# Merging the blocks of a triangular inverse earlier and in place, inside a hand-ordered hybrid decoder layer

## The chip, the cores and the metric

The kernel runs on one NeuronCore of a Trainium2 chip. Its metric is the device time of one execution in microseconds (us), the median of several runs. Below, PE is TensorE's matmul, PEld its weight load, DVE VectorE, ACT ScalarE, POOL GpSimd, and SP the queue that issues most DMAs (SPq its issuing instructions).

## The reference

One decoder layer on 512 tokens of width 1024. A normed input is projected once; half of the result goes to block-sparse attention with 8 heads of 64, the other half to a chunked gated DeltaNet with 8 heads of 64; both join in an output projection, and a squared-ReLU MLP of width 4096 follows. The part that matters here is the DeltaNet, with 8 chunks of 64 tokens for each head:

```python
qc, kc, vc = to_chunks(q), to_chunks(k), to_chunks(v)
decay = jnp.exp(jnp.where(causal, g_cum[..., :, None] - g_cum[..., None, :], -jnp.inf))
k_beta = kc * bc[..., None]
m = jnp.where(strict, jnp.einsum('bhnid,bhnjd->bhnij', k_beta, kc) * decay, 0.0)
a_mat = m + jnp.eye(C)
rhs = jnp.concatenate([vc * bc[..., None], k_beta * jnp.exp(g_cum)[..., None]], axis=-1)
uw = lax.linalg.triangular_solve(a_mat, rhs, left_side=True, lower=True, unit_diagonal=True)
u, w = uw[..., :dh], uw[..., dh:]
...
def step(state, xs):
    u_c, w_c, q_c, k_c, a_c, gl = xs
    v_new = u_c - jnp.einsum('bhck,bhkv->bhcv', w_c, state)
    o = jnp.einsum('bhck,bhkv->bhcv', q_c, state) + jnp.einsum('bhcs,bhsv->bhcv', a_c, v_new)
    state = state * gl[..., None, None] + jnp.einsum('bhck,bhcv->bhkv', k_c, v_new)
    return state, o
```

So each 64x64 unit triangular matrix is inverted, applied to the keys and the values, and then a state is carried through the chunks one after the other.

## The kernel before, in words

**Stages.** The input is normed and transposed (`pre_norm`, to about 20 us). The input projection (`projections`) runs 24 items of 128 columns and one wide item of 512, in the order of the string `ORDER`: k, q, v and z are the DeltaNet's pairs of heads 0 to 3, x and y the queries and keys of attention's pairs, and w its values. Each item has 24 products of 128x512 into one of two banks `ps_mm`, three for each of eight slices, since a float32 product is made of high and low halves (`mm3`). A weight slice is loaded into one of two buffers `w_raw` (L200, SP), cast to the high half on ACT (L205), and its low half is made on DVE or POOL (L206; the string `LO` says which). The bank is then evacuated by a stream of its own (`take_k`, `take_q`, `take_v`, `take_z`, `take_a`): for k, q and v a convolution with one pass on ACT (L485) and three on DVE (L488).

**The DeltaNet.** `chunks` makes for each pair of heads the matrices `NT` and `AT`. `inverse` loads the 32x32 diagonal blocks of `NT` through DRAM (`d_n`) with one block on each partition, inverts them by 31 pairs of DVE operations (L880, L881), and stores the inverses to `d_u` and their transposes to `d_t` (L885, L886). `scan` begins with the merge of two 32x32 blocks to one 64x64 inverse: it clears a buffer `UT` (L892, POOL), loads the transposes into `uap` (L897) and the blocks into `UT` (L900), makes 128 products of 32x32 (p1, L909), copies them (L913), makes 128 more (p2, L922), and writes them into `UT` (L926). Then come, for each pair of heads, the keys times a factor, `kB` (L934, POOL, one buffer), and their products with `UT` (L941), from which `LWQ` is filled (L943). The scan itself is eight steps (L981 to L1006), two yields each, in which the state `S` goes through DVE (L999, L1000). `finish_o` norms the outputs, waits for all of z0 to z3, transposes them and writes `mg_h` and `mg_l`.

**Attention.** `scores` and `values` work pair by pair with the keys `kt` (one buffer) and the queries `pt`. `output` then multiplies the joined halves (`mg`, `ma`) with the output weights `wo`; the MLP follows from about 313 us.

**What sets the order.** All of these are Python generators in one planner, `Weave`. Its clock `now` moves on by each product's columns, and each stream says at every yield how long it wants to wait, by a default in `WAIT`, or by an entry of `DELAY` under the stream's name and count ("merge.2" is the second yield of `merge`), or it waits for a mark that another stream sets. Among the streams that are ready the one of the lowest `RANK` goes first. This fixes the order of TensorE's instructions for good. The other engines are ordered by a list scheduler, in which `LEAD` and `PRIO` raise a stream's priority.

`scan` is spawned only when the inverse, the last chunks and all four values are marked, after the projections' pool is closed:

```python
    weave.run({"inverse", "chunks3", "v0", "v1", "v2", "v3"})
    sP.close()
    sc = pool("scan", 2, stack=sA, side="right")
    spawn(RANK["scan"], scan(), LEAD["scan"])
```

`big` buffers (14 of 128x2048) and `big_x` buffers (4 of the same size) are handed on when their last reader is done. `UT`, `inv`, `pt`, `LWQ` are `big`; `picks`, `kraw`, `ma_h`, `ma_l`, and later `mg_h` and `mg_l` are `big_x`.

Of the kernel before, what the change touches and what calls it, by code (L numbers as in the profile page):

```python
# [19 lines left out]
WAIT = {'h': 0.26, 'conv_k': 5.48, 'k': 6.88, 'conv_q': 8.11, 'q': 1.52, 'conv_v': 12.72, 'v': 2.29, 'z': 11.49, 'ab': 0.67, 'g': 9.16, 'scalars': 55.01, 'r_in': 0.0, 'r_out': 30.56, 'kk': 3.56, 'kk_out': 93.91, 'gl': 0.0, 'qk': 13.83, 'va': 1.36, 'a': 6.03, 'row': 1.56, 'rows': 4.29, 'pv': 2.34, 'att': 1.98, 'inverse': 0.76, 'merge': 6.6, 'p1': 2.26, 'p2': 223.99, 'w': 1.15, 'vn': 1.06, 'state': 0.64, 'o_in': 5.67, 'o': 1.23, 'wo': 1.48, 'wo_out': 0.86, 'normed3': 7.36, 'normed': 18.07, 'n': 2.53, 'up': 2.92, 'sums': 0.12, 'turned': 11.21, 'pv0': 3.36, 'wv': 3.58}  # L20

RANK = {'chunks': 5, 'inverse': 3, 'scan': 2, 'scores': 5, 'values': 4, 'finish_o': 2, 'take': 1}
LEAD = {'chunks': 30, 'inverse': 100, 'scan': 100, 'scores': 0, 'values': 0, 'finish_o': 100, 'take': 300, 'take_a': 100}
# [1612 lines left out]
```

## Time and profile before

| | us |
|---|---|
| median of three runs | 636.75 (636.13 to 636.93) |
| the profiled execution, its own time | 639.11 |
| its span, first to last instruction | 637.3 |
| the part ahead of the MLP (`w_up`'s weights in groups 2 to 7, `w_down`) | about 313 |
| TensorE's products, busy | 620.8 |
| VectorE, busy | 484.4 |
| ScalarE, busy | 370.3 |
| GpSimd, busy | 136.1 |

The profiled execution is one run, with 11091 instructions; a stretch's idle TensorE time is the stretch's length less the busy time. A busy TensorE is not always one at full speed: the granted clock is given beside it.

### The profile page before, as it was taken

Reading aid. Unit: us, or ns where it says so; the run is one execution under the profiler, and the core shown is the slowest. Engines: PE = TensorE matmul, PEld = TensorE weight load, DVE = VectorE, ACT = ScalarE, POOL = GpSimd, SP = SyncE. Lnnn points to the kernel's source line nnn. Section 1 sums busy time; section 2 is a strip of 40 time slices with the busy share of each in tenths; the row PEclk is TensorE's granted clock in tenths of the full one; section 3 lists DMA queues with packets and bytes.
Section 4 is the critical chain, followed back from the end, with each engine's and each line's share of the span. In section 5 each row is a group of like instructions: output and inputs, shape, how many; then the busy total and the mean of one; then the engine's idle time right before and its main releaser. Section 6 shows DMA issues by size and latency. Waiting matters only on the chain.

```text
span 637.3 us, 11091 instructions
## 1 busy us (share of the span) xinstructions
PE 620.8 (97%) x4291; PEld 535.8 (84%) x4291; DVE 484.4 (76%) x725; ACT 370.3 (58%) x620; POOL 136.1 (21%) x173
## 2 busy tenths in 40 slices
PE   9999999999989998999999999999999999999996
PEld 8777878888878876888898999999998888887884
DVE  4688887998735777947875578878789888887776
ACT  6385575445748656854325585556755666665661
POOL 4335430011334222002412311231211220000001
PEclk9999999999979999999999999999999999999999
DMA  6421335334371124724399998999999999867503
GB/s 223 131 76 65 101 100 143 107 102 146 113 120 37 41 61 138 247 96 166 117 361 248 175 296 241 255 262 233 280 257 340 298 291 285 261 212 298 180 0 133
DMA packets 61270, 115.26 MB, mean 181 GB/s; under 512 B 15862, under 2 KB 35449, under 8 KB 60834
## 3 DMA queue, kind: packets, MB, share of 16 engines
q1 hardware_dynamic: 43228, 84.93, 40.0%
q0 software_dynamic: 17696, 29.36, 22.1%
q8 instruction: 34, 0.56, 0.4%
q10 hardware_dynamic: 294, 0.27, 0.1%
q14 instruction: 18, 0.15, 0.1%
HBM read 106.65 MB, written 35.15 MB: 222 GB/s over the span
## 4 chain that ended last, share of the span: by engine, by line
PE 81%; DVE 6%; DMA 5%; ACT 3%; POOL 1%; issue 1%; SPq 1%; POOLq 0%; DVEq 0%; ACTq 0%
PE ps_mm L148 40%; PE ps_g L148 22%; PE ps_a L148 16%; DMA wo_raw<-in_w_out 1%; PE ps_a L152 1%; DMA xx<-in_x 1%; PE ps_g L152 1%; DVE conv L488 1%; DMA wd<-d_T 1%; DVE S L999 1%; DMA nb<-in_pre_mix 1%; DMA uap<-d_t 1%; DVE S L1000 1%; POOL oss L243 1%; SPq L900 1%
## 5 line engine op out<-in xcount | busy, mean ns | idle before, releaser
L181 ACT CAST wdh<-wd 128x1024 fp32r<-128x1024 f32 x53 | 55.6, 1050 | 51.2 <-PE ps_mm L148 23.6
L182 DVE TENSOR_TENSOR u_l<-w,u_h 128x1024 fp32r<-128x1024 f32 x46 | 56.2, 1224 | 37.9 <-ACT u_h L181 37.9
L182 DVE TENSOR_TENSOR wdl<-wd,wdh 128x1024 fp32r<-128x1024 f32 x53 | 64.9, 1225 | 22.8 <-ACT wdh L181 22.7
L181 ACT CAST u_h<-w 128x1024 fp32r<-128x1024 f32 x46 | 47.8, 1044 | 57.2 <-PE ps_a L148 19.8
L148 PE MATMUL ps_mm<-hT_h,w_hi 128*128 128x512 f32 (+1 forms) x192 | 76.4, 403 | 0.2 <-ACT hT_h L314 0.2
L148 PE MATMUL ps_mm<-hT_h,w_lo 128*128 128x512 f32 (+1 forms) x192 | 72.9, 385 | 0.0
L148 PE MATMUL ps_mm<-hT_l,w_hi 128*128 128x512 f32 (+1 forms) x192 | 72.6, 383 | 0.0
L1306 POOL DMA_DIRECT2D d_T<-in_w_down x32 | 33.1, 1034 | 143.6 <-DMA d_T<-in_w_down 82.3
L205 ACT CAST w_hi<-w_raw 128x512 fp32r<-128x512 f32 x56 | 34.8, 622 | 37.0 <-PE ps_mm L148 15.9
L206 POOL TENSOR_TENSOR w_lo<-w_raw,w_hi 128x512 fp32r<-128x512 f32 x21 | 27.2, 1294 | 97.2 <-ACT w_hi L205 94.2
L148 PE MATMUL ps_mm<-wdh,u_h 128*128 128x512 f32 x116 | 45.2, 390 | 0.0
L148 PE MATMUL ps_mm<-wdl,u_h 128*128 128x512 f32 x116 | 45.1, 389 | 0.0
L148 PE MATMUL ps_mm<-wdh,u_l 128*128 128x512 f32 x116 | 45.1, 389 | 0.0
L148 PEld LDWEIGHTS ps_mm<-hT_h,w_lo 128*128 128x128 f32 x192 | 35.8, 189 | 7.5
L148 PEld LDWEIGHTS ps_mm<-hT_h,w_hi 128*128 128x128 f32 x192 | 36.0, 190 | 6.6 <-issue 0.5
L148 PEld LDWEIGHTS ps_mm<-hT_l,w_hi 128*128 128x128 f32 x192 | 36.1, 190 | 5.4
L182 DVE TENSOR_TENSOR u_l<-f,u_h 128x1024 fp32r<-128x1024 f32 x28 | 34.1, 1218 | 0.0
L148 PE MATMUL ps_g<-wdh,u_h 128*128 128x512 f32 x80 | 31.2, 390 | 0.4 <-DVE y L1480 0.4
L148 PE MATMUL ps_g<-wdh,u_l 128*128 128x512 f32 x80 | 31.1, 389 | 0.0
L148 PE MATMUL ps_g<-wdl,u_h 128*128 128x512 f32 x80 | 31.1, 389 | 0.0
L206 DVE TENSOR_TENSOR w_lo<-w_raw,w_hi 128x512 fp32r<-128x512 f32 x35 | 24.4, 696 | 8.2 <-ACT w_hi L205 7.1
L488 DVE SCALAR_TENSOR_TENSOR conv<-ps_mm,cw,conv 128x511 f32<-128x511 f32 (+2 forms) x36 | 26.8, 746 | 4.1 <-ACT conv L485 3.4
(461 smaller groups left out, 1867.4 us busy)
## 6 DMA issues: line engine op xcount, KB each, us to landing
d_T<-in_w_down POOLq DMA_DIRECT2D x48, 512.0 KB, 10.8
wd<-d_T SPq DMA_DIRECT2D x32, 512.0 KB, 6.2
w<-in_w_up SPq DMA_DIRECT2D x28, 512.0 KB, 7.7
wd<-in_w_down SPq DMA_DIRECT2D x24, 512.0 KB, 6.7
w_raw<-in_w_in SPq DMA_DIRECT2D x46, 256.0 KB, 2.7
wo_raw<-in_w_out SPq DMA_DIRECT2D x16, 256.0 KB, 2.9
d_T<-d_T POOLq DMA_DIRECT2D x8, 512.0 KB, 11.0
xx<-in_x SPq DMA_DIRECT2D x4, 512.0 KB, 7.4
```

The lines of the kernel that those rows point to most:

```text
L148: nc.tensor.matmul(o, l, r, **kw)
L152: nc.tensor.transpose(o, i, ident[:k, :k])
L181: nc.scalar.copy(hi, src)
L182: tt(lo, src, f32(hi), op=OP.subtract)
L205: nc.scalar.copy(hi, raw)
L206: (sub or tt)(lo, raw, f32(hi), op=OP.subtract)
L243: nc.gpsimd.tensor_tensor(r, r, m, op=OP.pow)
L488: stt(c[:, s:], p[:, :512 - s], cw[:, ft, j:j + 1], c[:, s:], op0=OP.mult, op1=OP.add)
L900: nc.sync.dma_start(z3(UT[32 * b:32 * b + 32, :, :, o:o + 32]), d_u[b].rearrange("z j i -> j z i"))
L999: tt(Sn[hs, :, hs], S[hs, :, hs], EGL[hs, :, n:n + 1].to_broadcast([64, 4, 64]), op=OP.mult)
L1000: tt(Sn[hs, :, hs], Sn[hs, :, hs], sp[n][cs, hh::2], op=OP.add)
L1306: nc.gpsimd.dma_start(d_T[t][k], block(b, second)[k], accum_op=OP.add, max_dma_last_dim=1024)
```

## The change

The merge leaves `scan` and becomes a stream of its own, `merge`, that waits for the mark "inverse"; the products with `kB` become a third stream, `weights_of_k`, that waits for "merged"; `scan` waits for "LW". `UT` is no longer a buffer of its own: once the inverse's two stores have left, its buffer is viewed as `UT`, and the six loads go into it. The lower left quarter, in which p1's result stands until p2 has read it, is cleared afterwards. `kB` gets one `big_x` buffer for all four pairs, and the keys of attention's pairs 1 and 2 another.

```diff
         def ev_k(ps):
-            kts[p] = at.tile([128, 2, 512], FR, name="kt", bufs=1)
+            if p in (0, 3):
+                kts[p] = at.tile([128, 2, 512], FR, name="kt", bufs=1)
+            else:
+                if p == 1:
+                    kt2.append(big_x("kt", (128, 2, 2, 512), FR))
+                kts[p] = kt2[0][:, p - 1]
...
+        merged.append(inv.rearrange("p a j i -> p (a j i)").rearrange("p (h t e) -> p h t e", h=8, t=4))
         iT = iN
         nc.vector.tensor_copy(iT, iU.rearrange("p j i -> p i j"))
...
-    def scan():
-        UT = big("UT", (128, 8, 4, 64))
-        nc.gpsimd.memset(UT, 0.0)
-        uap = [sc.tile([128, 4, 4, 32], FT, name="uap", tag="ot", bufs=4) for _ in range(2)]
+    def merge():
+        yield "inverse"
+        UT = merged[0]
         z3 = lambda a: a.rearrange("p h t i -> p (h t) i")
+        left, right = ([slice(64 * c + o, 64 * c + o + 32) for c in range(2)] for o in (0, 32))
+        first, second = slice(0, 32), slice(32, 64)
         for c in range(2):
-            for z in range(2):
-                nc.sync.dma_start(z3(uap[z][64 * c:64 * c + 32]), d_t[2 * c, 16 * z:16 * z + 16].rearrange("z j i -> j z i"))
-        for b in range(4):
-            o = 32 * (b % 2)
-            nc.sync.dma_start(z3(UT[32 * b:32 * b + 32, :, :, o:o + 32]), d_u[b].rearrange("z j i -> j z i"))
+            nc.sync.dma_start(z3(UT[left[c], :, :, second]), d_t[2 * c].rearrange("z j i -> j z i"))
+        for c in range(2):
+            nc.sync.dma_start(z3(UT[right[c], :, :, second]), d_u[2 * c + 1].rearrange("z j i -> j z i"))
+        for c in range(2):
+            nc.sync.dma_start(z3(UT[left[c], :, :, first]), d_u[2 * c].rearrange("z j i -> j z i"))
         yield WAIT["merge"]
...
             for c in range(2):
-                b = slice(64 * c + 32, 64 * c + 64)
-                nc.scalar.copy(uap[z][b], p1[b])
+                nc.scalar.copy(UT[right[c], zs, :, first], p1[right[c]])
...
             for c in range(2):
-                a = slice(64 * c, 64 * c + 32)
-                nc.scalar.mul(z3(UT[a, 4 * z:4 * z + 4, :, 32:64]), z3(p2[a]), -1.0)
-        yield WAIT["p2"]
+                nc.scalar.mul(UT[left[c], zs, :, second], p2[left[c]], -1.0)
+        for c in range(2):
+            nc.gpsimd.memset(UT[right[c], :, :, first], 0.0)
+        mark("merged", WAIT["p2"])
+
+    def weights_of_k():
+        yield "merged"
+        UT = merged[0]
+        kBs = big_x("kB")
...
-                kB = sc.tile([128, 512], FT, name="kB", bufs=1).rearrange("p (t h e) -> p t h e", t=4, h=2)
+                kB = kBs[:, p].rearrange("p (t h e) -> p t h e", t=4, h=2)
...
+        mark("LW")
+
+    def scan():
+        yield "LW"
+        UT = merged[0]
...
     spawn(RANK["inverse"], inverse(), LEAD["inverse"])
+    spawn(RANK["inverse"], merge(), LEAD["scan"])
+    spawn(RANK["inverse"], weights_of_k(), LEAD["scan"])
```

The planner's numbers are drawn anew as well:

```diff
-RANK = {'chunks': 5, 'inverse': 3, 'scan': 2, 'scores': 5, 'values': 4, 'finish_o': 2, 'take': 1}
-LEAD = {'chunks': 30, 'inverse': 100, 'scan': 100, 'scores': 0, 'values': 0, 'finish_o': 100, 'take': 300, 'take_a': 100}
+RANK = {'chunks': 5, 'inverse': 2, 'scan': 2, 'scores': 2, 'values': 3, 'finish_o': 5, 'take': 1}
+LEAD = {'chunks': 30, 'inverse': 100, 'scan': 300, 'scores': 0, 'values': 30, 'finish_o': 300, 'take': 0, 'take_a': 0}
...
-ORDER = 'k0 k1 q0 q1 q2 k2 q3 k3 x0 y0 z0 w x1 v2 v0 y1 v1 v3 x2 y2 z2 x3 z1 y3 z3'
+ORDER = 'k0 k1 q0 q1 q2 k2 q3 k3 x0 y0 z0 x1 y1 w v2 v1 v0 v3 z2 x2 y2 y3 x3 z1 z3'
...
-LO = 'ppvvpvpvpppvvvvppvvvvvvvvvvvvvvvpvvppvvvppppvppvppvvvpvvvvvvvvvv'
+LO = 'pppppvpvpppvpvvpvvvvvvvvvvvvvvvvvvvvvvpvvvvvvvvvvpppvpvvppppvvvv'
```

`DELAY` goes from 415 to 455 entries: 380 keys are in both, 181 of them with another value; 75 are new and 35 are dropped. Among the new ones are "merge.2" 32.73, "merge.3" 1.39, "merged" 1.4 and "LW" 0.09. `PRIO` goes from 53 entries to 96; the seven numbers of `START` (planned times of the first streams) and most defaults in `WAIT` change ("vn" 1.06 to 1.27, "state" 0.64 to 2.07).

More of the change, by code (lines that the diff above doesn't have):

```diff
@@ L18 @@
 EPS = 1e-6
-WAIT = {'h': 0.26, 'conv_k': 5.48, 'k': 6.88, 'conv_q': 8.11, 'q': 1.52, 'conv_v': 12.72, 'v': 2.29, 'z': 11.49, 'ab': 0.67, 'g': 9.16, 'scalars': 55.01, 'r_in': 0.0, 'r_out': 30.56, 'kk': 3.56, 'kk_out': 93.91, 'gl': 0.0, 'qk': 13.83, 'va': 1.36, 'a': 6.03, 'row': 1.56, 'rows': 4.29, 'pv': 2.34, 'att': 1.98, 'inverse': 0.76, 'merge': 6.6, 'p1': 2.26, 'p2': 223.99, 'w': 1.15, 'vn': 1.06, 'state': 0.64, 'o_in': 5.67, 'o': 1.23, 'wo': 1.48, 'wo_out': 0.86, 'normed3': 7.36, 'normed': 18.07, 'n': 2.53, 'up': 2.92, 'sums': 0.12, 'turned': 11.21, 'pv0': 3.36, 'wv': 3.58}
-RANK = {'chunks': 5, 'inverse': 3, 'scan': 2, 'scores': 5, 'values': 4, 'finish_o': 2, 'take': 1}
-LEAD = {'chunks': 30, 'inverse': 100, 'scan': 100, 'scores': 0, 'values': 0, 'finish_o': 100, 'take': 300, 'take_a': 100}
+WAIT = {'h': 1.11, 'conv_k': 6.12, 'k': 6.74, 'conv_q': 25.48, 'q': 1.67, 'conv_v': 17.21, 'v': 0.53, 'z': 12.14, 'ab': 0.0, 'g': 10.7, 'scalars': 99.29, 'r_in': 0.68, 'r_out': 4.98, 'kk': 3.96, 'kk_out': 50.39, 'gl': 0.76, 'qk': 67.34, 'va': 1.56, 'a': 28.87, 'row': 2.12, 'rows': 0.03, 'pv': 2.61, 'att': 0.84, 'inverse': 0.49, 'merge': 0.83, 'p1': 4.55, 'p2': 43.21, 'w': 2.23, 'vn': 1.27, 'state': 2.07, 'o_in': 1.73, 'o': 5.78, 'wo': 3.8, 'wo_out': 0.5, 'normed3': 8.54, 'normed': 16.52, 'n': 9.64, 'up': 5.6, 'sums': 0.32, 'turned': 41.6, 'pv0': 6.53, 'wv': 0.39}
+RANK = {'chunks': 5, 'inverse': 2, 'scan': 2, 'scores': 2, 'values': 3, 'finish_o': 5, 'take': 1}
+LEAD = {'chunks': 30, 'inverse': 100, 'scan': 300, 'scores': 0, 'values': 30, 'finish_o': 300, 'take': 0, 'take_a': 0}
 FILL = (8, 3, 0)
@@ L28 @@
 VBANKS = ('mm', 'mm', 'a', 'a')
-START = (1.86, 1.69, 7.77, 14.48, 18.11, 17.11, 68.08)
-ORDER = 'k0 k1 q0 q1 q2 k2 q3 k3 x0 y0 z0 w x1 v2 v0 y1 v1 v3 x2 y2 z2 x3 z1 y3 z3'
-DELAY = {"projections.84": 0.19, "turned3": 1.48, "inverse": 1.14, "inverse.14": 3.11, "projections.173": 0.0, "values.15": 5.25, "scan.3": 0.96,
[58 rows of a table removed]
-PRIO = {'weights_out.16': 20, 'projections.11': 0, 'chunks3.7': 60, 'output.56': 60, 'projections.54': 20, 'output.58': 20, 'output.59': 0, 'projections.75': 60, 'projections.71': 20, 'scores.19': 400, 'output.50': 400, 'projections.117': 0, 'projections.3': 0, 'projections.70': 150, 'inverse.26': 150, 'output.46': 150, 'output.24': 400, 'projections.16': 60, 'scores.6': 400, 'inverse.17': 60, 'x3.1': 400, 'output.11': 150, 'values.40': 150, 'projections.13': 0, 'projections.9': 60, 'scores.9': 400, 'scan.2': 60, 'inverse.9': 60, 'output.68': 150, 'projections.93': 60, 'scores.34': 400, 'weights_out.12': 150, 'w0.1': 400, 'output.51': 150, 'scores.15': 0, 'inverse.25': 150, 'scan.15': 0, 'output.53': 20, 'projections.196': 20, 'projections.83': 60, 'chunks1.3': 20, 'values.18': 400, 'v0.1': 150, 'projections.34': 0, 'output.66': 150, 'scan.18': 400, 'chunks2.4': 150, 'chunks2.5': 20, 'projections.31': 400, 'scores.39': 0, 'y2.1': 20, 'z3.1': 60, 'output.19': 60}
@@ L93 @@
-LO = 'ppvvpvpvpppvvvvppvvvvvvvvvvvvvvvpvvppvvvppppvppvppvvvpvvvvvvvvvv'
+START = (3.9, 0.0, 12.81, 10.48, 11.79, 28.38, 73.43)
+ORDER = 'k0 k1 q0 q1 q2 k2 q3 k3 x0 y0 z0 x1 y1 w v2 v1 v0 v3 z2 x2 y2 y3 x3 z1 z3'
+DELAY = {"projections.84": 0.0, "inverse": 2.6, "inverse.14": 3.11, "projections.173": 0.0, "values.15": 4.71, "merged": 1.4, "inverse.9": 1.17,
[64 rows of a table added]
+PRIO = {'chunks3.7': 60, 'projections.54': 20, 'output.58': 20, 'output.59': 0, 'projections.75': 60, 'scores.19': 400, 'projections.117': 60, 'output.24': 20, 'scores.6': 400, 'output.11': 150, 'values.40': 150, 'projections.9': 150, 'output.68': 150, 'projections.93': 60, 'scores.34': 400, 'output.51': 150, 'inverse.25': 150, 'scan.9': 0, 'output.53': 60, 'projections.196': 20, 'projections.83': 60, 'v0.1': 150, 'projections.34': 0, 'scan.12': 400, 'chunks2.5': 400, 'projections.31': 400, 'output.17': 400, 'projections.46': 20, 'projections.76': 400, 'output.47': 0, 'normed2.1': 20, 'projections.107': 0, 'projections.199': 60, 'output.9': 20, 'inverse.14': 20, 'output.25': 150, 'projections.25': 20, 'inverse.19': 60, 'projections.200': 60, 'values.31': 150, 'inverse.16': 150, 'chunks1.5': 0, 'output.43': 400, 'projections.136': 150, 'output.27': 150, 'scalars.3': 20, 'inverse.3': 400, 'projections.142': 20, 'projections.8': 400, 'scores.15': 0, 'weights_up.9': 0, 'output.30': 150, 'projections.29': 0, 'output.49': 150, 'scores.4': 0, 'projections.32': 20, 'weights_of_k.4': 0, 'projections.146': 60, 'output.26': 60, 'scan.14': 0, 'weights_out.17': 400, 'weights_up.4': 0, 'projections.188': 400, 'projections.14': 20, 'projections.71': 60, 'scores.28': 400, 'projections.156': 400, 'projections.154': 20, 'projections.38': 60, 'scores.26': 0, 'output.42': 60, 'weights_out.5': 400, 'scores.29': 400, 'output.52': 400, 'projections.150': 60, 'projections.119': 0, 'inverse.24': 60, 'scan.19': 400, 'v2.1': 400, 'x1.1': 400, 'scan.17': 150, 'projections.7': 150, 'weights_up.7': 20, 'projections.153': 150, 'projections.15': 20, 'z0.1': 400, 'scan.7': 400, 'w1.1': 150, 'projections.124': 60, 'projections.184': 20, 'output.55': 20, 'q2.2': 20, 'projections.30': 400, 'q1.1': 150, 'scores.9': 0, 'projections.127': 60}
@@ L725, in layer @@
     d_e = dram.tile([8, 640], FT, name="d_e")
-    pts, kts, vals = {}, {}, []
+    pts, kts, kt2, vals = {}, {}, [], []
     def bias():
@@ L866, in values @@
             mark(f"att{p}", WAIT["att"])
+    merged = []
     def inverse():
@@ L907, in scan @@
                     for c in range(2):
-                        a, b = slice(64 * c, 64 * c + 32), slice(64 * c + 32, 64 * c + 64)
-                        mm(p1[b, h, t], NT[a, 4 * z + h, t, 32:64], uap[z][a, h, t], start=True, stop=True,
+                        mm(p1[right[c], h, t], NT[left[c], 4 * z + h, t, second], UT[left[c], 4 * z + h, t, second], start=True, stop=True,
                            tile_position=(64 * c, 64 * c + 32))
             for c in range(2):
-                b = slice(64 * c + 32, 64 * c + 64)
-                nc.scalar.copy(uap[z][b], p1[b])
+                nc.scalar.copy(UT[right[c], zs, :, first], p1[right[c]])
         mark("p1")
@@ L916, in scan @@
         for z in range(2):
+            zs = slice(4 * z, 4 * z + 4)
             p2 = bank(shape=(128, 4, 4, 32))
@@ L920, in scan @@
                     for c in range(2):
-                        a, b = slice(64 * c, 64 * c + 32), slice(64 * c + 32, 64 * c + 64)
-                        mm(p2[a, h, t], uap[z][b, h, t], UT[b, 4 * z + h, t, 32:64], start=True, stop=True,
+                        mm(p2[left[c], h, t], UT[right[c], 4 * z + h, t, first], UT[right[c], 4 * z + h, t, second], start=True, stop=True,
                            tile_position=(64 * c + 32, 64 * c))
             for c in range(2):
-                a = slice(64 * c, 64 * c + 32)
-                nc.scalar.mul(z3(UT[a, 4 * z:4 * z + 4, :, 32:64]), z3(p2[a]), -1.0)
-        yield WAIT["p2"]
+                nc.scalar.mul(UT[left[c], zs, :, second], p2[left[c]], -1.0)
[6 more added lines that the diff above has]
+        kBs = big_x("kB")
         for z in range(2):
```

1 line of the change is left out of this document (added), and 122 rows, old and new, of the table DELAY.

## The prediction

> **What bounds the kernel now.** I read the page first, for the shares, the clock line and the chain.
>
> ```profile
> span 637.3 us, 11091 instructions
> ...
> PE 620.8 (97%) x4291; PEld 535.8 (84%) x4291; DVE 484.4 (76%) x725; ACT 370.3 (58%) x620; POOL 136.1 (21%) x173
> ...
> PEclk9999999999979999999999999999999999999999
> ...
> PE 81%; DVE 6%; DMA 5%; ACT 3%; POOL 1%; issue 1%; SPq 1%; POOLq 0%; DVEq 0%; ACTq 0%
> ```
>
> TensorE is busy for 97% of the span and carries 81% of the chain. The change neither adds nor removes a product, so it can only win time in which TensorE stands still or runs slowly. The clock line has one mark under 9, in the twelfth of 40 slices (15.93 us each, so 175 to 191 us). The table by stretches then says where TensorE loses time. Its columns are the stretch, its length, then busy us and count for each engine, the granted clock, the DMA share and GB/s.
>
> ```profile
> core 0: us, PE busy (x) PEld busy (x) DVE busy (x) ACT busy (x) POOL busy (x), PEclk, DMA share, GB/s
> ...
> 180.85:184.27 3.42, 1.77 (x18) 1.05 (x19) 1.22 (x2) 1.61 (x3) 1.27 (x1) 1.00 1.05 169
> 184.27:191.09 6.82, 6.82 (x134) 6.04 (x131) 0.82 (x2) 3.85 (x7) 0.00 (x0) 0.50 0.13 43
> 191.09:194.50 3.41, 3.41 (x134) 2.93 (x133) 2.56 (x5) 2.51 (x6) 0.00 (x0) 1.00 0.03 7
> ...
> 204.20:240.77 36.57, 33.81 (x511) 27.88 (x506) 25.80 (x54) 23.17 (x44) 8.91 (x15) 1.00 0.18 52
> ...
> 252.30:259.60 7.30, 6.06 (x43) 4.90 (x43) 6.72 (x18) 7.19 (x19) 0.00 (x0) 1.00 0.34 103
> ```
>
> ```profile
> 176.40:180.80 4.40, 4.40 (x28) 3.83 (x27) 1.52 (x5) 1.21 (x2) 3.67 (x4) 1.00 1.43 171
> 30.00:100.00 70.00, 68.83 (x456) 54.49 (x455) 60.47 (x131) 44.99 (x105) 28.80 (x33) 1.00 0.30 85
> 100.00:180.00 80.00, 80.00 (x399) 67.31 (x399) 66.11 (x156) 43.86 (x92) 14.88 (x13) 1.00 0.46 127
> ```
>
> Idle TensorE, length less busy: 1.65 us in 180.85 to 184.27, then 6.82 us at half the clock, which is 3.41 us of lost work; 2.76 us in the scan (204.20 to 240.77); 1.24 us after the last projection (252.30 to 259.60); 1.17 us in 30 to 100; nothing in 100 to 180. The waits between 172 and 262 us (us in total, times, longest) and the chain there (start, length, what) name the causes:
>
> ```profile
> POOL kB L934 <- PE ps_g L148: 12.8, 1, 12.8
> ...
> PE ps_g L148 <- DVE S L1000: 2.8, 3, 1.4
> ...
> PE ps_g L148 <- DMA uap<-d_t: 1.6, 2, 0.9
> ...
> PEld ps_g L148 <- POOL kB L934: 0.4, 1, 0.4
> ```
>
> ```profile
> 174.66 0.58 SPq L900
> ...
> 179.02 0.53 SPq L897
> ...
> 179.60 0.98 SPq L897
> ...
> 180.63 3.43 DMA uap<-d_t
> ...
> 184.11 3.53 PE ps_g L148 x126
> ...
> 191.76 2.14 PE ps_g L148 x128
> ```
>
> The first merging products (p1) stand in TensorE's fixed order and wait for `uap`, whose loads SP issues only from 179 us, behind the four loads of `UT`. Yet the inverse was ready long before:
>
> ```profile
> L874 POOL MEMSET inv<- x1: 952/952/952, 86.5 to 86.5; 128x1024 f32 x1
> ...
> L886 SPq DMA_DIRECT2D d_t<-inv x1: 327/327/327, 145.2 to 145.2; - x1
> ...
> DMA to landing us min/median/max: 2.7/4.1/4.2
> ```
>
> Its last store leaves at 145.2 and lands by 149.4. The merge waits 25 us more because `scan`, in which it stands, is spawned only when the values v0 to v3 are through and the projections' pool is closed; v3's transposes start at 174.67:
>
> ```profile
> 174.67 1.04 PE L152 MATMUL ps_g<-ident,vt 128*128 128x128 f32 x8
> ```
>
> **The change, part by part.** Times are differences to the profiled run (639.11 us, span 637.3); the three timed runs have their median 2.36 us lower, at 636.75, and I carry the difference over.
>
> *The merge's place.* `merge` now waits for the mark "inverse" alone, so its loads can leave at about 150, and the planner puts p1 32.73 us of planned time behind them ("merge.2"). That is about 183, the place where p1 stands now, but with loads that land some 25 us earlier. The wait of 1.65 us in 180.85 to 184.27 goes: -1.65. What is late next is nothing I can see: the inverse would have to end 25 us later. This is bounded by 0 and -1.65.
>
> *The clock.* The half clock follows that thin stretch directly, and the next products of the same form (p2: 128 in 2.14 us, inside 191.09 to 194.50) ran at 1.00. So thin products among dense ones do not lower it; the wait does. With the wait gone: -3.41, between 0 and -3.41. I take the whole, since p2's row is the nearest one. [...]
>
> *The loads.* Eight (four of `UT`, four half-sized of `uap`) become six of the larger kind.
>
> ```profile
> L900 SPq DMA_DIRECT2D UT<-d_u x4: 577/770/1098, 174.7 to 177.3; - x4
> L148 PE MATMUL ps_g<-UT,uap x128: 191/191/212, 191.7 to 193.7; 32*32 32x32 f32 x128
> L926 ACT ACTIVATE UT<-ps_g x4: 587/589/592, 193.0 to 195.5; 32x512 f32<-32x512 f32 x4
> L892 POOL MEMSET UT<- x1: 1813/1813/1813, 170.3 to 170.3; 128x2048 f32 x1
> ```
>
> Six at 0.77 are 4.6 us on SP's queue, moved from 174.7 to about 150, ahead of weight loads (L200) that wait behind them. They also wait for the stores: up to 4.2 us more of a blocked queue. Where the burst stands now, TensorE stayed busy for 4.40 of 4.40 us, so I take 0. If the two buffers of raw weights don't cover, the loss is at most these 8.8 us less the 4.40 us that were demonstrably covered, +4.4. A gain is excluded, because the old place cost nothing on TensorE.
>
> *The buffer.* The memset of `UT` (1.81 us, POOL) goes; two of 32 partitions by 1024 come, each like the inverse's own at 0.95, so 1.9 us on POOL behind p2. They stand between p2 and the first product with kB, beside the four evacuations of 0.589 (2.4 us) that this product also waits for, so 0; without that cover +1.9. Queued behind them on POOL are the kB products and low halves of weights (21 of 56 before, 20 after). Evacuations of p1 now write the merged buffer with a stride, as those of p2 already do: 0.
>
> *kB.* With four slots in place of one, POOL's 12.8 us wait ends; it hid behind projections except for the 0.4 us of a weight load. -0.4, between 0 and -0.4. `mg_h` and `mg_l` now wait for kB and the key buffer; their first writer comes after z3, far behind: 0.
>
> *Keys of pairs 1 and 2.* Their own buffer means no evacuation waits for the scores of the pair before. No TensorE wait names one: 0, at best -0.5.
>
> *Delays, ranks and order.* Of the 380 delays that both have, 181 differ; the scan's sixteen steps have 26.7 us of planned gaps in place of 21.2 (sums of the `scan` delays, "vn" and "state" where none is given). More other work between two steps means less of the 2.8 us wait for S. I take half, -1.4, bounds 0 and -2.8. Everything else in the new order can win at most the idle 1.17 and 1.24 us (-2.4), and can lose about what the same kind of order loses in the scan and behind it now, 2.76 + 1.24 = +4.0. I take 0.
>
> Sum: -1.65 - 3.41 - 0.4 - 1.4 = -6.9. The profiled run would come to 632.2, the median to 636.75 - 6.9 = 629.9, rounded to **630**. All the gains together (-1.65 - 3.41 - 0.4 - 0.5 - 2.8 - 2.4 = -11.2) give 625.6.
>
> **The rivals.**
>
> *The clock is not won* (17%). Either p1, p2 and the kB products make a thin stretch at their new place, or the timed runs, 2.36 us under the profiled one, lacked the dip already. Against it: p2's row at 1.00 and the narrow spread of the runs. 629.9 + 3.4 = 633.3.
>
> *The tail is laid bare* (12%). x3 and y3 now come ahead of z1 and z3, and scores and values have rank 2 and 3, so attention may be done when z3 ends, and the chain behind z3 has nothing beside it:
>
> ```profile
> 253.48 0.60 ACT zs L554
> ...
> 254.57 0.53 ACT t L556
> ...
> 255.12 0.69 DVE zs L557
> ...
> 256.29 0.66 DVE om L1031
> ...
> 259.72 1.39 PE ps_mm L148 x6
> ```
>
> Of the 7.30 us, only the 16 transposes would remain (0.13 each by the row of eight in 1.04), 2.1 us, so 5.2 us idle in place of 1.24: +4.0, 633.9. Against it: the delays of pair 3's last scores grow too ("scores.35" to "scores.38").
>
> *Nothing comes of it* (10%). The new order loses in the scan what the merge wins: 636.75.
>
> *Slower: the evacuations fall behind* (13%). The lead of the projections' evacuations falls from 300 (100 for attention) to 0, while inverse, merge and scan have 100 to 300. There are two banks of `ps_mm`; twelve of the projections hold one through an ACT pass and three DVE passes. If one cast and one subtraction of weights slip in ahead of each, the bank comes free later by their durations:
>
> ```profile
> L488 DVE SCALAR_TENSOR_TENSOR conv<-ps_mm,cw,conv x36: 735/746/751, 28.9 to 167.8; 128x511 f32<-128x511 f32 x12, 128x510 f32<-128x510 f32 x12, 128x509 f32<-128x509 f32 x12
> ```
>
> ```profile
> L205 ACT CAST w_hi<-w_raw x56: 601/621/667, 8.8 to 301.0; 128x512 fp32r<-128x512 f32 x56
> L206 DVE TENSOR_TENSOR w_lo<-w_raw,w_hi x35: 680/686/980, 26.5 to 303.3; 128x512 fp32r<-128x512 f32 x35
> ```
>
> 0.62 + 0.69 = 1.3 us, times twelve, is 15.7 us at most. It makes the kernel slower once the mean wait is over (638.0 - 629.9) / 12 = 0.68 us; at 0.9 us the time is 640.7. Against it: no wait of TensorE for a bank stands in the trace now, with 100 to 180 us fully busy.
>
> **How the numbers follow.** My forecast holds 43%, with 5% more for the case that all the gains come (about 626). 0.2% (1.3 us) is about what a measurement of this kernel can tell from no change, so faster means under 635.5 and slower over 638.0. Faster: 43 + 5 + 17 + 12, less 2 for the upper ends of the last two, 75%. Same: 10 + 2 = 12%. Slower: 13%. The range runs from 625 (the sum of all gains) to 637.5, which leaves out the slower case and little below; the forecast's own range is 626 to 633.
>
> **What would show it.** p1 without a wait for a load, and no granted clock of 0.5 between 100 and 300 us: the first two terms. Loads of `UT` before 160 us on SP. TensorE's wait for S under 2 us: the scan's term. The last projection's end and the first output product less than 7.3 us apart, or an idle stretch there: the tail. Waits of `ps_mm` products for conv or zs between 30 and 250 us: the slower case. The part behind 313 us should keep its length; if it does not, my reading of where the change acts is wrong. The forecast falls if new waits of TensorE before 260 us add up to more than 5 us.

## The result, and the profile after

The changed kernel takes 641.9 us (median of 8 runs, 640.11 to 643.57) against 636.88 for the kernel before (8 runs, 636.13 to 639.07), 5.0 us more. By the means of the runs it is 1.0069 times as long (4.4 us), 95% interval 1.0049 to 1.0089. The forecast was 630, and the measured time lies above its whole range of 625 to 637.5. The profiled execution took 642.16 us with a span of 640.3, 3.05 us more than the profiled one of before. The new code stands at other lines: the products at L154 (before L148), the evacuations of `pt` and `kt` at L749 and L763, the loads of the merge at L911 to L915, `kB` at L955.

The page of the changed kernel, for the shares, the clock and the chain:

```profile
span 640.3 us, 11084 instructions
PE 618.9 (97%) x4291; PEld 533.0 (83%) x4291; DVE 485.7 (76%) x730; ACT 369.0 (58%) x620; POOL 129.1 (20%) x169
PEclk8999999799999999999999999999999999999998
PE 80%; DVE 9%; DMA 4%; ACT 4%; issue 2%; SPq 1%; POOL 1%; POOLq 0%; DVEq 0%; ACTq 0%
```

TensorE's share of the chain is about what it was, DVE's grew from 6% to 9%. The low mark of the clock line has moved from the twelfth slice to the eighth, and a small one (8) stands in the first. The stretches show the trade; first those of the kernel before, then those of the changed one (columns as in the prediction).

```profile
100.00:124.00 24.00, 24.00 (x112) 20.02 (x112) 19.96 (x57) 11.69 (x28) 0.00 (x0) 1.00 0.46 131
...
180.00:200.00 20.00, 18.36 (x366) 14.94 (x364) 8.12 (x17) 13.75 (x28) 5.40 (x6) 0.83 0.33 68
200.00:262.00 62.00, 58.01 (x705) 47.83 (x705) 43.91 (x94) 41.28 (x84) 16.39 (x22) 1.00 0.27 82
```

```profile
113.57:120.65 7.08, 1.33 (x6) 0.52 (x4) 6.72 (x17) 2.99 (x5) 0.00 (x0) 0.75 0.73 185
120.65:124.00 3.35, 3.35 (x8) 2.67 (x9) 3.11 (x8) 0.00 (x0) 0.00 (x0) 0.51 0.00 0
150.00:165.00 15.00, 15.00 (x345) 12.88 (x343) 7.08 (x12) 10.26 (x19) 3.24 (x4) 1.00 0.47 96
180.00:200.00 20.00, 20.00 (x102) 16.86 (x101) 15.10 (x26) 12.15 (x24) 0.00 (x0) 1.00 0.30 92
200.00:262.00 62.00, 61.00 (x666) 50.35 (x665) 46.94 (x104) 43.00 (x93) 14.80 (x20) 1.00 0.30 87
```

From 180 to 262 us idle TensorE falls from 1.64 + 3.99 us to 0 + 1.00, and the half clock at 184 is gone: this is the gain that the prediction wanted. But in 113.57 to 120.65 TensorE stands 5.75 us where before had none, and works at half the clock after it: at 0.51 products of 128x512 start 0.43 us apart, at 1.00 (from 124.30 us on) 0.23 us. Its waits in the changed kernel (us in total, times, longest), from 60 to 180 and from 180 to 262 us:

```profile
PE ps_mm L154 <- DVE kt L763: 4.3, 1, 4.3
PE ps_mm L154 <- DVE pt L749: 1.5, 1, 1.5
PE ps_a L154 <- DVE kt L763: 1.2, 1, 1.2
```

```profile
PE ps_g L154 <- DVE S L1025: 0.6, 2, 0.4
```

The waits for `uap` are gone, that for `S` fell from 2.8 to 0.6 us. The first two lines are one place, seen in the order of time on TensorE and on DVE (start, length, what, idle time before it):

```profile
115.43 0.47 PE L154 MATMUL ps_mm<-w_hi,hT_h 128*128 128x512 f32 x1 [1.47 <-DVE pt L749]
...
120.65 0.76 PE L154 MATMUL ps_mm<-w_hi,hT_h 128*128 128x512 f32 x1 [4.28 <-DVE kt L763]
```

```profile
108.75 0.21 DVE L893 TENSOR_TENSOR pr<-inv 128x31 f32<-128x31 f32 x1 [4.05 <-DMA inv<-d_n]
...
114.59 0.69 DVE L749 SCALAR_TENSOR_TENSOR pt<-ps_mm,pt 64x512 fp32r<-64x512 f32 x1
...
119.81 0.69 DVE L763 TENSOR_TENSOR kt<-ps_mm,kt 64x512 fp32r<-64x512 f32 x1
```

These are the first products of `w`. That item needs four banks at once, by `VBANKS` two of `ps_mm` and two of `ps_a`; every other item needs one. In the new order it comes directly behind x1 and y1, whose results still fill both `ps_mm` banks. DVE empties them late, between steps of the inverse and low halves of weights; before that it stood 4.05 us, because the next instruction in its order, the inverse's first step, waited for a load.

p1 came early, not at 183 (instances, shortest/median/longest ns, first and last start):

```profile
L154 PE MATMUL ps_g<-inv,NT x128: 191/191/212, 154.9 to 157.0; 32*32 32x32 f32 x128
...
L911 SPq DMA_DIRECT2D inv<-d_t x2: 319/438/557, 147.9 to 148.3; - x2
...
L915 SPq DMA_DIRECT2D inv<-d_u x2: 806/826/847, 150.3 to 151.2; - x2
```

The 32.73 planned us between loads and p1 were 7 us on the chip. The loads had landed all the same, because the wait at 116 us held TensorE back; in w_first, g_banks and gk below, which lack this wait, TensorE reaches p1 at 146 us and waits for them.

### The profile page after: what moved, and what is told of

It reads as the page before. It is cut to its first block, busy times and chain, and to the rows that moved or that the text cites. A ratio compares the mean times of both kernels' runs of the same rounds, so it can differ in the third digit from the quotient of the medians.

```text
span 640.3 us, 11084 instructions
## 1 busy us (share of the span) xinstructions
PE 618.9 (97%) x4291; PEld 533.0 (83%) x4291; DVE 485.7 (76%) x730; ACT 369.0 (58%) x620; POOL 129.1 (20%) x169
## 4 chain that ended last, share of the span: by engine, by line
PE 80%; DVE 9%; DMA 4%; ACT 4%; issue 2%; SPq 1%; POOL 1%; POOLq 0%; DVEq 0%; ACTq 0%
PE ps_mm L154 39%; PE ps_g L154 22%; PE ps_a L154 16%; PE ps_a L158 2%; DVE conv L494 1%; PE ps_g L158 1%; DMA w_raw<-in_w_in 1%; DMA t<-in_w_up 1%; DMA inv<-d_n 1%; DVE w_lo L212 1%; DMA d_n<-NT 1%; DVE xs L1160 1%; DVE L L809 0%; DVE kt L763 0%; DVE inv L894 0%
## 5 line engine op out<-in xcount | busy, mean ns | idle before, releaser
L154 PE MATMUL ps_mm<-hT_h,w_hi 128*128 128x512 f32 (+1 forms) x192 | 76.0, 401 | 0.1
L154 PE MATMUL ps_mm<-hT_h,w_lo 128*128 128x512 f32 (+1 forms) x192 | 72.6, 383 | 0.0
L154 PE MATMUL ps_mm<-hT_l,w_hi 128*128 128x512 f32 (+1 forms) x192 | 72.4, 382 | 0.0
L154 PE MATMUL ps_mm<-wdh,u_h 128*128 128x512 f32 x116 | 45.3, 390 | 0.0
L154 PE MATMUL ps_mm<-wdh,u_l 128*128 128x512 f32 x116 | 45.1, 389 | 0.0
L154 PE MATMUL ps_mm<-wdl,u_h 128*128 128x512 f32 x116 | 45.1, 389 | 0.0
L154 PEld LDWEIGHTS ps_mm<-hT_h,w_lo 128*128 128x128 f32 x192 | 35.6, 188 | 7.4
L212 DVE TENSOR_TENSOR w_lo<-w_raw,w_hi 128x512 fp32r<-128x512 f32 x40 | 28.4, 709 | 17.2 <-ACT w_hi L211 15.6
L154 PEld LDWEIGHTS ps_mm<-hT_h,w_hi 128*128 128x128 f32 x192 | 35.7, 188 | 6.5 <-issue 0.5
L154 PEld LDWEIGHTS ps_mm<-hT_l,w_hi 128*128 128x128 f32 x192 | 35.8, 189 | 5.3
L212 POOL TENSOR_TENSOR w_lo<-w_raw,w_hi 128x512 fp32r<-128x512 f32 x16 | 20.7, 1294 | 66.6 <-ACT w_hi L211 65.2
L154 PE MATMUL ps_g<-wdh,u_h 128*128 128x512 f32 x80 | 31.2, 390 | 0.4 <-DVE y L1507 0.4
L154 PE MATMUL ps_g<-wdl,u_h 128*128 128x512 f32 x80 | 31.1, 389 | 0.0
L154 PE MATMUL ps_g<-wdh,u_l 128*128 128x512 f32 x80 | 31.1, 389 | 0.0
```

The costliest lines, as they stand in the source:

```text
L154: nc.tensor.matmul(o, l, r, **kw)
L212: (sub or tt)(lo, raw, f32(hi), op=OP.subtract)
```

## The experiments

Three theories were tried. *Order*: `w` behind x1 and y1 is the loss. *Place*: p1 stands too early, so loads and kB are the next wait. *Rival*: the new code itself costs. In the recorded expectations the bank theory is Order, the two-waits theory is Order and Place together, and the structure theory is Rival. The load theory blames the 4.05 us that DVE stands for the inverse's load, and the fit theory says that any edit that moves the order costs time, since the delays were fitted to one order. All ratios are to the kernel before on the same chip, with their 95% intervals.

**w first in the changed kernel's order.**

```diff
-ORDER = '... z0 x1 y1 w v2 ...'
+ORDER = '... z0 w x1 y1 v2 ...'
```

> The changed kernel with the wide item w ahead of x1 and y1, as it stood before; everything else as changed. Bank theory: behind x1 and y1, w takes both ps_mm banks at once and TensorE waits 1.5 + 4.3 us for the evacuation of y1, and the 6.8 us of half clock behind it cost 3.4 us more; with w first no such wait stands between 95 and 130 us, and the time falls by 6 to 9 us, to 633 to 636. Load theory (DVE stands 4.0 us before the inverse's first operation, for the load of inv, and everything late there comes from that): the stand stays, whatever is next in DVE's order is late by it, and TensorE waits elsewhere: 639 to 643. Structure theory (the merge's new place costs the time): 640 to 643.

1.0134 (1.0116 to 1.0153). The wait of `w` for its banks is gone, but p1 came at 146 us, before its loads, waited 4.7 us, and 13.65 us at half clock followed. The median, 646.6 us, lies outside all three ranges, and the order's share is not told by this run alone.

**w in other banks.**

```diff
-VBANKS = ('mm', 'mm', 'a', 'a')
+VBANKS = ('g', 'g', 'a', 'a')
```

> The changed kernel, same order of items, but w's first two accumulations go to two of the three ps_g banks in place of the two ps_mm banks. Bank theory: the wait at 114 to 121 us goes with its half clock, 6 to 9 us less: 633 to 636. Load theory: the weights' low halves stand behind the same 4.0 us on DVE, TensorE waits for them instead: 638 to 643. Structure theory: 640 to 643.

1.0058 (1.0041 to 1.0074). Again no wait at 114 us and p1 too early. The median of 642.0 us lies in the ranges of the load and structure theories, but the wait that makes it is p1's. The chain in this kernel goes through the inverse's store and load:

```profile
142.82 3.03 DMA d_t<-inv
...
146.28 2.69 DMA inv<-d_t
...
149.02 2.98 PE ps_g L154 x121
```

```profile
150.00:156.00 6.00, 6.00 (x144) 5.31 (x141) 1.69 (x3) 3.85 (x7) 0.00 (x0) 0.50 0.51 74
156.00:163.40 7.40, 7.40 (x100) 6.66 (x95) 1.38 (x2) 4.24 (x7) 3.92 (x5) 0.50 0.01 2
```

So the wait for the banks had hidden this one. These two stretches are in half clock throughout.

**The inverse's load ahead of its first step.** Its load became a stream of its own, 8 planned us ahead of the inverse.

> The changed kernel, with the inverse's load in a stream of its own and the first inverse operation put 8 us of planned time behind it. DVE then should not stand before it. Load theory: the evacuations of x1 and y1 come 4 us earlier, TensorE's wait at 114 to 121 us falls from 6.1 to 2 us or less and the half clock goes: 634 to 637. Bank theory: a part of the wait stays, since y1's bank is asked for as soon as y1 ends and its two ACT and two DVE passes take 2.5 us at the least: 636 to 640. Structure theory: 640 to 643.

1.0123 (1.0106 to 1.0141), above all the ranges, and it tells little: the edit also moved products in TensorE's order, DVE still stood 3.4 us for the load, the wait of 4.3 us stayed, and others grew.

**p1 later in the changed kernel, alone and with each cure for `w`.**

```diff
-"merge.2": 32.73
+"merge.2": 55.0
```

> The changed kernel with the merge's first products put 55 us of planned time behind its loads in place of 32.73 (p1 then stands some 15 us further on in TensorE's order); all else as changed. Two-waits theory: the wait for y1's bank at 114 to 121 us costs the changed kernel its time, and only because of it do the merge's loads land in time for p1; with p1 later alone the bank's wait and its half clock stay: 640 to 644, as the changed kernel. Place theory (it is p1's early place alone that costs): 632 to 636.

> Both at once: w's first two accumulations in ps_g banks, and the merge's first products 55 us of planned time behind its loads. Two-waits theory: with either alone gone the other costs the time (with the ps_g banks alone p1 came 2.5 us before its load and 13.6 us ran at half the clock); with both gone neither is left, and the time is 8 to 10 us under the changed kernel: ratio to before 0.990 to 0.997. Fit theory (any edit that shifts the order against the hand-set delays costs 5 us or more, whatever it removes): 1.005 or more.

> The wide item w ahead of x1 and y1, and the merge's first products 55 us of planned time behind its loads. Two-waits theory: w first alone let p1 come 4.9 us before its load, with 13.6 us at half the clock; with p1 later both go: ratio to before 0.991 to 0.998. Fit theory: 1.005 or more.

1.0239 (1.0205 to 1.0273), 1.0097 (1.0068 to 1.0127) and 1.0371 (1.0340 to 1.0402). The first lies above both its ranges; in the other two the two-waits theory fell, and the fit theory's 1.005 or more came. In the second neither the banks nor p1 are waited for any more, but TensorE waits anew for the state S (3.0 us) and for `vn`, the new values of a step of the scan (2.5). In the third:

```profile
PE ps_a L158 <- DVE xs L1160: 6.9, 1, 6.9
PE ps_a L154 <- DVE mins L809: 6.8, 1, 6.8
```

Moving p1 reorders everything behind it, and none of the places tried suits the other numbers as well. Two mended waits do not add up when other steps move too.

**The new code with before's numbers**, p1 by 32.73 planned us, and by 70, which puts it where the kernel before has it (183 us).

> The new code (merge and kB products in streams of their own, in the inverse's buffer, keys of pairs 1 and 2 in another) with the numbers of before: order, ranks, leads, delays, priorities; only the merge's place is as in the changed kernel (32.73 us of planned time behind the inverse). Bank and load theory: w stands ahead of x1 as before, no wait there; the waits for uap (1.65 us) and the half clock behind them (3.4 us) go: 630 to 633. Structure theory: slower than before, over 638.

> The new code with the numbers of before, and p1 70 us of planned time behind its loads, which is where the planner of before put it (71 us behind the inverse). This is what the prediction priced: loads early, p1 where it stood. Two-waits theory: the wait for uap and the half clock of before are gone and p1 waits for nothing: ratio 0.988 to 0.996. Structure theory (memset of POOL, kB behind it, or the handed-on buffers cost by themselves): over 1.005, with a TensorE wait for POOL's kB at the first kB product, as with p1 early (4.8 us).

1.0440 (1.0423 to 1.0457) and 1.0010 (0.9992 to 1.0027). At the early place POOL's memset waits for p2 and kB behind it, and TensorE waits 4.8 us for kB. At the late place the wait for `uap` and the half clock behind it are gone (granted clock 0.998 over the profiled run), as forecast, and yet nothing is won: neither theory's range holds the ratio. Its waits at 149 to 157 us, the stretch (first in the kernel before, then here), and the two groups that explain it:

```profile
PE ps_mm L86 <- DVE conv L426: 1.3, 1, 1.3
PE ps_a L86 <- DVE kt L695: 0.8, 1, 0.8
PE ps_g L90 <- DVE vt L430: 0.6, 1, 0.6
```

```profile
147.00:156.50 9.50, 9.50 (x46) 7.84 (x45) 8.71 (x15) 4.07 (x7) 0.00 (x0) 1.00 0.32 102
...
147.00:156.50 9.50, 7.39 (x33) 5.22 (x31) 9.47 (x9) 2.86 (x5) 8.79 (x7) 1.00 0.78 129
```

```profile
L760 DVE TENSOR_TENSOR V<-V 128x512 fp32r<-128x512 f32 x1 | 1.5, 1546 | 0.0
...
L426 DVE SCALAR_TENSOR_TENSOR conv<-ps_mm,cw,conv 128x511 f32<-128x511 f32 x1 | 0.7, 749 | 0.4 <-ACT conv L423 0.4
```

With four slots, all eight POOL products of kB and kdec run in a row (145.4 to 155.8 us). Beside them DVE finishes 9 operations in place of 15: of the six that read two operands from SBUF five take 1.53 to 1.55 us and one 0.87, in place of 0.68 to 0.69; the convolution's, which read PSUM, take 0.73 to 0.75, as in the kernel before.

**One slot for kB again, there and in the changed kernel.**

```diff
-                kB = kBs[:, p].rearrange("p (t h e) -> p t h e", t=4, h=2)
+                kB = kBs[:, 0].rearrange("p (t h e) -> p t h e", t=4, h=2)
```

> The changed code with the numbers of before and p1 at before's place (structure_late, ratio 1.001), with one change: the kB products share one slot of the same buffer again, so three of the four kB and three of the four kdec products on POOL come behind p2, each behind the TensorE products of the pair before. Theory (POOL's products slow VectorE's operations that read two operands from SBUF, and that eats the gain): between 145 and 157 us those VectorE operations fall from about 1.53 to about 0.69 us each except beside the one kB and one kdec product that stay (some 2.5 us), TensorE's waits there for conv (1.3), kt (0.8) and vt (0.6) go, and the time falls by 2 to 3 us: 0.995 to 0.998 of before. Rival (the waits at 149 to 157 us come of delays that were fitted to another order, and POOL beside them is chance): the waits stay near 2.7 us and the ratio near 1.001. A third outcome: the waits at 149 to 157 go, but TensorE now waits for kB behind p2, up to 1.1 us for each of two pairs, and the ratio stays within 0.002 of 1.

> The changed kernel with one slot for kB, one edit. Between 90 and 99 us the eight POOL products kB and kdec (9.0 us together) stand beside VectorE operations that take 1.50, 1.25 and 0.90 us in place of 0.69, 0.75 and 0.16, 2.05 us more in all. Theory (that lateness is carried to the evacuations that TensorE waits for at 113 to 120 us): those operations return to their usual lengths but for one, TensorE's wait of 1.2 us for kt at 93.8 goes, the waits in front of w (10 us) shrink by 1 to 2 us, and the ratio falls from 1.007 to 1.000 to 1.005. Rival (VectorE catches up by 104 us, where it stands 4 us for the inverse's load anyway): the waits in front of w keep their length and the ratio stays at 1.005 to 1.009.

In the first, with TensorE's order unchanged, the stretch is whole again and a low half takes its 683 ns:

```profile
147.00:156.50 9.50, 9.50 (x46) 7.86 (x45) 7.15 (x13) 3.45 (x6) 0.83 (x1) 1.00 0.78 153
```

```profile
L144 DVE TENSOR_TENSOR w_lo<-w_raw,w_hi 128x512 fp32r<-128x512 f32 x2 | 1.4, 683 | 0.0
```

```profile
PE ps_a L86 <- DVE mins L741: 1.5, 1, 1.5
PE ps_a L90 <- DVE mins L741: 1.4, 2, 0.8
```

So POOL's products beside DVE are what made those waits. But the ratio is 1.0006 (0.9991 to 1.0021), not to be told from structure_late: 2.9 us of waits for `mins` (of attention's scores) came at 163 to 166 us and behind p2 (195). In the changed kernel the same edit gave 1.0032 (1.0017 to 1.0046) in place of 1.0069; the two intervals, from two chips, just overlap. TensorE's order is the same; the waits for `kt` at 93 us and `pt` at 113 us fell to 0.4 and 0.8 us, while the longest, 4.3 us, stayed. The theory's number came, the place only in part.

**The order alone, in the kernel before.**

```diff
-ORDER = '... z0 w x1 v2 v0 y1 v1 v3 ...'
+ORDER = '... z0 x1 y1 w v2 v0 v1 v3 ...'
```

> Before with one edit: in the fixed order of projections y1 comes ahead of w, so w directly follows x1 and y1, as in the changed kernel. Theory (w's first two accumulations need the two ps_mm banks of x1 and y1, which the VectorE evacuations still hold): a wait of TensorE for pt or kt in front of w, 3 to 6 us together, and half a clock behind it (up to 3.4 us more): 1.005 to 1.015 of before. Rival (the order alone does no harm; what makes the evacuations late in the changed kernel is VectorE's own stand of 4 us for the inverse's load and the lead of the inverse): a wait under 1.5 us, no half clock behind it, and a ratio of 0.998 to 1.003.

1.0084 (1.0064 to 1.0105), with this wait of TensorE and this stretch:

```profile
PE ps_mm L148 <- DVE kt L752: 3.9, 1, 3.9
```

```profile
112.00:116.30 4.30, 0.41 (x3) 0.05 (x1) 4.07 (x10) 1.35 (x3) 0.00 (x0) 0.86 0.67 183
```

A half clock of 6.83 us begins there. This order costs about 5 us alone, as much as the whole change within the two intervals. It needs neither the new code nor DVE's stand of 4 us: here DVE stood 1.54. Nor does it need the lower lead of attention's evacuations, which is 100 here and 0 in the changed kernel; what that lead adds was not run alone.

**All numbers of the change in before's code.**

> Before's code, its merge inside scan and its buffers, with all of the changed kernel's numbers (waits, ranks, leads, starts, order, delays, priorities; those of merge and of the products with kB carried to the steps of scan that hold the same work; the 32.73 us in front of p1 have no counterpart and are left out). Theory (the new order of projections is what costs, and the new code is what wins): the wait in front of w and half a clock behind it stand as in the changed kernel, and the merge's own wait for uap stays as before, so 1.010 to 1.020 of before. Rival (the numbers are good and the new code costs): 0.995 to 1.002.

1.0571 (1.0545 to 1.0596). The sign is the theory's (`kt` 4.3 us, `uap` 5.6, S 3.3), the size is not: some 36 us come together from more waits than the theory named and the half clocks behind them, and the numbers do not carry over to before's code.

**Start times, and the cures together.** `START` of the kernel before (after_start); with the banks and the slot (gks); with "merge.2" at 37 besides (gks_37); the last two with the changed start times (gk, gk_37).

> The changed kernel with before's seven start times, nothing else; TensorE's products stand in the same order. In the changed kernel TensorE stands 1.9 us at 6.1 us for the first xs, and a half clock of 3.41 us follows (1.7 us of lost work); before has neither. Theory (the later start time of the first loads makes both): they go, and the time falls by 2 to 3.6 us, to 1.0015 to 1.004 of before in place of 1.0069. Rival (the arrival of x sets that wait, and the start times only place it): the wait stays near 1.9 us or comes back as two shorter ones, and the ratio stays at 1.005 to 1.008.

> The changed kernel with w's first two accumulations in the banks ps_g (as in g_banks), one slot for kB (as in after_kb1) and before's start times (as in after_start); TensorE's order is that of g_banks, in which p1 stands early and waits 2.5 us for its load, with 13.65 us of half clock behind. If the causes add up: g_banks' 1.0058, less 0.0037 for kB, less 0.003 to 0.0045 for the start: 0.998 to 1.000. Rival (they hide one another, and the next wait takes the time won): 1.002 to 1.006.

> gks with 37.0 in place of 32.73 us of planned time in front of p1, which puts twelve more products between the inverse's end and p1 (some 4 us) and reorders what follows. Theory (p1's wait for its load is what is left): no wait of p1, so 2.5 us and the half clock behind it (13.65 us, 6.8 us of lost work) go: 0.985 to 0.992 of before. Rival (the other numbers fit one place of p1 only, as with 55 us, where S, vn and ph were waited for anew): new waits of 3 us or more between 160 and 260 us, and a ratio of 0.996 to 1.005.

> The changed kernel with w's first two accumulations in the banks ps_g (as in g_banks) and one slot for kB (as in after_kb1); start times as changed, TensorE's order that of g_banks. If the two causes add up: g_banks' 1.0058 less 0.0037 is 1.002 (1.000 to 1.004); the start stays as in the changed kernel, and p1 still waits about 3 us for its load, with a half clock of 10 us or more behind it. Rival (the time that the slot wins is taken by p1's wait for its load, which ends at a fixed time): 1.004 to 1.007, and a longer wait of p1.

> gk with 37.0 in place of 32.73 us of planned time in front of p1. gks_37 had no half clock after 40 us and no wait of p1, but lost 8 us of waits and 10 us of half clock before 30 us to the start times, which are the changed kernel's own here. Theory (w's banks, POOL beside VectorE and p1's loads make up the loss): no wait over 2 us and no half clock between 30 and 300 us, and 0.994 to 1.001 of before. Rival (the reordering behind p1 loses more, since its other numbers fit one place of p1): no half clock, but shorter waits that sum up, and 1.002 to 1.010.

1.0178 (1.0148 to 1.0207), 1.0169 (1.0140 to 1.0197) and 1.0203 (1.0173 to 1.0232): the first-named theory fell in all three. Before's start times take the 1.9 us at 6 us away and bring two other waits, in after_start:

```profile
PE ps_mm L154 <- POOL w_lo L212: 3.8, 1, 3.8
PE ps_mm L154 <- DVE hT_l L317: 2.2, 1, 2.2
```

The wait at 6 us comes and goes: with the same start times it was 1.9 us in the changed kernel, 1.0 in gk and absent in g_banks, and with before's code and start times it was absent in the kernel before and 0.7 in two_queues below, whose edit acts only at 178 us. It is a part of the difference between the two profiled runs (1.24 us of idle time before 20 us, and 3.41 us at half clock); whether the change makes it more frequent is open. With the changed start times, gk gave 1.0041 (1.0022 to 1.0060), by its interval not to be told from g_banks nor from after_kb1, and gk_37 1.0054 (1.0032 to 1.0076), at a granted clock of 0.993 in the profiled run, with 0.9 us of waiting for p1's loads left, and several new waits of 0.6 to 1.2 us. None of these orders gets below before.

In the stretch of the loss, though, the two cures do what they should. The same 44 us of the kernel before, the changed kernel, after_kb1, g_banks and gk, in this order:

```profile
80.00:124.00 44.00, 43.85 (x267) 35.60 (x267) 38.18 (x100) 24.95 (x64) 5.73 (x8) 1.00 0.43 117
80.00:124.00 44.00, 36.81 (x222) 28.69 (x223) 36.44 (x92) 23.11 (x60) 14.08 (x16) 0.92 0.42 115
80.00:124.00 44.00, 38.62 (x226) 29.93 (x225) 36.90 (x92) 22.98 (x60) 7.52 (x10) 0.92 0.42 112
80.00:124.00 44.00, 42.84 (x257) 34.24 (x256) 37.59 (x91) 23.83 (x62) 14.09 (x16) 1.00 0.45 123
80.00:124.00 44.00, 43.65 (x261) 34.93 (x261) 37.34 (x92) 24.77 (x63) 7.52 (x10) 1.00 0.45 125
```

Idle TensorE is 0.15, 7.19, 5.38, 1.16 and 0.35 us: the banks and the slot of kB together take away 6.84 of the 7.04 us that the change adds there. In gk 2.80 us of idle time come back from 140 to 150 us, where p1 waits for its loads.

**The wait for `uap` alone, in the kernel before.** Two of its four loads are issued by ScalarE.

```diff
-                nc.sync.dma_start(z3(uap[z][64 * c:64 * c + 32]), ...)
+                (nc.sync, nc.scalar)[c].dma_start(z3(uap[z][64 * c:64 * c + 32]), ...)
```

> Before with one edit: of the four loads of uap, the two of the second pair of blocks are issued by ScalarE in place of SP, so the loads that the first products p1 need leave at about 178.0 and 179.0 us in place of 179.0 and 180.2; ScalarE stands idle from 178.0 to 180.1 in before. TensorE's order is untouched. Theory (the wait of 1.65 us makes the half clock, and both count in the time): the wait falls to 0.5 us or less, no half clock at 184 us, all runs at a granted clock of about 0.997, and a ratio of 0.995 to 0.998. Rival (thin products make the half clock, or other waits take the time won): a granted clock of 0.993 and a ratio of 0.999 to 1.001. If the half clock is in only some runs of before, the gain lies between the two, and the spread of the runs shrinks to that of before's runs at 0.997 (634.8 to 636.7 us).

0.9987 (0.9969 to 1.0004). The edit did not take the wait away:

```profile
PE ps_g L148 <- DMA uap<-d_t: 2.3, 1, 2.3
```

```profile
L897 ACTq DMA_DIRECT2D uap<-d_t x2: 310/338/367, 177.4 to 178.5; - x2
...
DMA to landing us min/median/max: 4.3/4.6/4.9
```

The first of ScalarE's loads left at 177.4 us, 1.6 us before the first of before. But the four loads took 4.6 us to land (median) in place of 3.4, and p1 began at 184.0 us in place of 183.1. An earlier issue was thus lost in a slower transfer; that the transfers around them caused this is argued, not shown. What the wait and the clock behind it are worth by themselves was not measured.

## Why the prediction was wrong, point by point

The sum went wrong in three terms: the order, put at 0, cost about 5 us; kB, put at -0.4, cost about 2; and the 3.41 us of the clock were not all there to be won from the median.

- **"Everything else in the new order ... I take 0", bounds to +4.0: this step failed.** The order of projections was read as if its items were alike. `w` takes both `ps_mm` banks at its start, and behind x1 and y1 that is 5.75 us of standing, with half a clock on the 3.35 us that follow (some 1.6 us lost: eight products at 0.43 us in place of 0.23). Alone it cost about 5 us in the kernel before (order_only), and with other banks for `w` the wait goes (g_banks). The bound was taken from the idle time of the scan, which has nothing to do with banks.
- **The slower rival had the engine right and the place wrong.** It spread 0.9 us over twelve items; it was one item that needs two banks at once. That "no wait of TensorE for a bank stands in the trace now" was true of an order in which `w` followed z0.
- **kB, -0.4: wrong in sign.** The four slots let POOL run ahead, beside DVE. One slot gave about 0.0037 of the time back in the changed kernel (some 2 us), and 1.81 us of idle TensorE from 80 to 124 us. Beside POOL's products in structure_late the DVE operations with two operands in SBUF took 1.53 us (one 0.87) in place of 0.68, the convolution's 0.75 in both kernels. In the changed kernel a low half took 1.50 us in place of 0.69, and a small cast of one operand 0.90 in place of 0.16. Why one operation is slowed and another is not, no run shows.
- **"That is about 183": wrong.** p1 stood at 154.9 us. Planned us are not us of the chip. p1's waiting for loads, which the change should have ended, was a few us away (the loads issued at 147.9 and 148.3 us take 2.1 us in the median, and p1 starts at 154.9) and came back in w_first, g_banks and gk.
- **The merge's place, -1.65: made, with luck.** p1 waits for nothing, 15.00 of 15.00 us busy. But it stands some 28 us earlier than forecast, and its loads were in time only because TensorE had been held up before.
- **The clock, -3.41: right for its place, mis-sized for the median.** The dip at 184 us went; in structure_late, where p1 waits for nothing either, all 12 runs have a granted clock of 0.996 to 0.999. But in the changed kernel a dip as long came at 117. And the sum took 3.41 us from a median of runs that, by their times, in part lack such a dip: of 23 runs of before on one chip, eight at a granted clock of 0.997 took 634.8 to 636.7 us, while those at 0.993, as in the profiled run, took 638.5 to 639.2. So about 2.8 us lie between their means; which stretch was at half clock in runs without a profile is not recorded. This is the second case of the rival with 17%.
- **Scan, -1.4: larger, within its bound of -2.8.** The wait for S fell by 2.2 us, idle time from 200 to 262 us by 2.99.
- **Loads and buffer, 0 each: held.** The memset waited 61.9 us on POOL for p2, and nothing on TensorE waited for it.
- **The part behind 313 us: kept its length, as forecast.** TensorE's idle time in the last 324.3 us is 6.96 us before and 7.11 after.

The changed kernel's loss is thus a gain of some 4.6 us of idle time in 180 to 262, and a larger loss, 7.04 us, in 80 to 124. The order's part of it is shown by order_only and g_banks, kB's by after_kb1, and gk, with both cured, stands only 0.35 us there. That they add up to the whole time is not shown: gk is still at 1.0041, and p1's wait for its load then stands in their place.

## What to carry to other kernels

When an order of work changes, list for each item how many buffers it needs at its start, and who frees them and when, before pricing the idle time that the old order has. A second buffer is not free where it lets one engine run ahead beside another that it slows (here from 0.68 to 1.53 us an operation): look which operations would then stand side by side. A wait that is taken away uncovers the next; before counting it as won, look how many us that next one is away.
